# Read-back additions inside and behind the last pair's first product, and more PSUM banks for the one-hot products

## The chip, the cores and the metric

The kernel runs on one core of a Trainium2 chip. The metric is the device time of one execution, in microseconds (us); lower is better. All times below count from the start of the profiled span. The engines are named as the profile names them: PE (TensorE, matrix products), DVE (VectorE), ACT (ScalarE), POOL (GpSimd) and SP (SyncE, which here issues most of the transfers).

## The reference

A trunk of two layers works on 512 tokens of width 1024. A layer first mixes tokens (attention, pooling and a dilated attention), and then adds a mixture of experts. The change lies in the second part. Each token goes to two of 32 experts:

```python
top_v, top_i = lax.top_k(el_sel, TOP_K)
top_w = jax.nn.softmax(top_v, axis=-1) * g_w[:, None]
...
for g in range(N_GROUPS):
    hid = jax.nn.silu(jnp.einsum('td,edf->tef', t, w1[g])) * jnp.einsum('td,edf->tef', t, w3[g])
    hid = hid * combine[:, g, :, None].astype(hid.dtype)
    y = y + jnp.einsum('tef,efd->td', hid, w2[g]).astype(jnp.float32)
...
x = x + ga2 * hier_moe(h, w_rg[l], b_rg[l], w_re[l], b_re[l], w1[l], w3[l], w2[l])
```

An expert has a hidden width of 256. The reference computes in float32.

## The kernel before, in words

The token tiles X[0] to X[3] (128 tokens each) stay on the chip. In the mixture, the 32 experts are worked on in 16 pairs (pair 0 to pair 15); a pair takes up to 64 tokens for each of its two experts, so one block of 128 slots. Per pair, PE does the first product (`stage1`, L1118: eight steps j, each over two experts, into bank 0 or 1), ACT applies silu (L1122), DVE multiplies in the gate and the token's weight (L1123, "gating" below), PE transposes the hidden rows (L1130), and does the second product (`down`, L1138: two halves of 512 columns into banks 2 and 3). After the first product stands a branch (L1186) for experts with more than 64 tokens; a longer list is worked on inside it.

How a pair's result reaches X differs. Pairs 0 to 12 scatter their rows to a table `y_d` in device memory, two rows per token. In pair 13, `fetch_back` (L1203) issues eight loads that bring the table back, two for each token tile, in the order of `TAIL` = 3, 0, 2, 1; and `add_back(m)` (L1208) is two DVE additions of 128x1024 that add the two loaded halves to X[m]. These are the row additions. The last three pairs (13 to 15, `direct`) don't use the table: their result is scaled (L1150) and split into a high and a low part (ACT L299, DVE L300), and PE multiplies it by a one-hot matrix `oh` (128 slots by 512 tokens, built by DVE from the slots' token numbers in L1158). `combine` returns four steps of this, one for each token tile: in a step, for each half of the columns, PE does L1164 and L1165 into a PSUM bank and DVE adds the bank to X (L1166).

The steps of pair 13 run inside the first product of pair 14, and those of pair 14 inside that of pair 15: after j = 2, 4 and 6, and the fourth behind the gating. The steps of pair 15 stand by themselves at the end of the layer. In layer 1 each of the last ones is followed by an output transfer (L1281).

In these last pairs the order on PE, ACT, DVE and POOL is the order in which the code is written; each engine takes its work in its order. In layer 0, instructions of layer 1's beginning are woven in between, among them the loads of small tables on POOL (L320, with `lam_a`), a small reduction on `lam_a` (L387 on DVE, L389 on ACT), fills (L251), and the split of the first weights (L299, L300 with 128x1024). These tables use buffers that the read-back rows had: `lam_a` has the one of tile 0's rows (`unit_173` in layer 0).

Of the kernel before, what the change touches and what calls it, by code (L numbers as in the profile page):

```python
# [79 lines left out]
def trunk(ctx: ExitStack, tc: tile.TileContext, I, out, dbg=None):  # L80
# [46 lines left out]
    slot_f = smallp.tile([128, 2, 16, 8], F32, name="slot_f")  # L127
# [41 lines left out]
    def release(key):  # L169
        held.pop(key).free()  # L170
# [904 lines left out]
    def moe(l, us, done):  # L1075
# [10 lines left out]
        def gather(dst, idx):  # L1086
            nc.gpsimd.indirect_dma_start(out=dst, out_offset=None, in_=xn_d,  # L1087
                                         in_offset=bass.IndirectOffsetOnAxis(ap=idx, axis=0),
                                         bounds_check=S - 1, oob_is_err=False)
# [5 lines left out]
        def rows_T(src, dst, *then, banks=(4, 5)):  # L1095
            v = src.rearrange("p (q j) -> p j q", j=8)
            for j in range(8):
                nc.tensor.transpose(PS[banks[j // 4]][:, 128 * (j % 4):128 * (j % 4) + 128], v[:, j, :], ident)  # L1098
                if j == 3 and then:
                    then[0]()  # L1100
            for j in range(8):
                p = PS[banks[j // 4]][:, 128 * (j % 4):128 * (j % 4) + 128]
                if j < 4:
                    nc.scalar.activation(dst[:, j, :], p, AF.Identity, bias=cols[:, SH2, j:j + 1],
                                         scale=cols[:, SC2, j:j + 1])
                else:
                    nc.vector.tensor_scalar(dst[:, j, :], p, cols[:, SC2, j:j + 1], cols[:, SH2, j:j + 1],  # L1107
                                            op0=OP.mult, op1=OP.add)
            if then:
                then[1]()  # L1110

        def stage1(pr, b, xT, comb, between=(), after=(2, 4, 6)):

            ph = PS[b]
            for j in range(8):
                for r in range(2):
                    ws = get(("wg", l, 2 * pr + r, j // 4)).rearrange("p (n j f) -> p j n f", n=2, j=4)
                    nc.tensor.matmul(ph[64 * r:64 * r + 64, :], xT[:, j, 64 * r:64 * r + 64], ws[:, j % 4],  # L1118
                                     start=j == 0, stop=j == 7, tile_position=(0, 64 * r))
                if j in after and between:  # L1120
                    between.pop(0)()
            nc.scalar.activation(sil[b], ph[:, 0:256], AF.Silu)  # L1122
            nc.vector.scalar_tensor_tensor(hid[b], ph[:, 256:512], comb, sil[b], op0=OP.mult, op1=OP.mult)  # L1123
            for f in between:
                f()

        def hidden_T(b, part=(0, 1)):
            hv = hid[b].rearrange("p (q j) -> p j q", j=2)
            for j in part:
                nc.tensor.transpose(PS[b][:, 128 * j:128 * j + 128], hv[:, j, :], ident)  # L1130
                nc.scalar.activation(hidT[b][:, j, :], PS[b][:, 128 * j:128 * j + 128], AF.Copy)  # L1131

        def down(pr, b, banks=(2, 3), each=None):
            w2 = [get(("w2", l, 2 * pr + r)).rearrange("p (j n d) -> p j n d", j=2, n=2) for r in range(2)]
            for n in range(2):
                for j in range(2):
                    for r in range(2):
                        nc.tensor.matmul(PS[banks[n]][64 * r:64 * r + 64, :], hidT[b][:, j, 64 * r:64 * r + 64],  # L1138
                                         w2[r][:, j, n, :], start=j == 0, stop=j == 1, tile_position=(0, 64 * r))
                if each:  # L1140
                    each(n)


        direct = lambda pr: pr >= 16 - DIRECT
# [12 lines left out]
        def combine(b, tf, banks=(6, 7), done=None):  # L1157
            nc.vector.tensor_scalar(oh.bitcast(F32R), iota, tf, None, op0=OP.is_equal)  # L1158

            def step(m, n):  # L1160
                p = PS[banks[(2 * m + n) % len(banks)]]
                cs = slice(512 * n, 512 * n + 512)
                o = oh[:, 128 * m:128 * m + 128].bitcast(F32R)
                nc.tensor.matmul(p, o, yh[b][:, cs].bitcast(F32R), start=True, stop=False)  # L1164
                nc.tensor.matmul(p, o, yl[b][:, cs].bitcast(F32R), start=False, stop=True)  # L1165
                nc.vector.tensor_tensor(X[m][:, cs], X[m][:, cs], p, op=OP.add)  # L1166
                if done:
                    done(m, cs)
            return [lambda m=m: [step(m, n) for n in range(2)] for m in range(NT)]
# [13 lines left out]
        def extra(pr, b):  # L1183

            n = blocks(pr)
            with tc.If(n > 1, label=f"extra{l}_{pr}"):  # L1186
                more(pr, b, slot_f[:, 0, pr, 1:2], slot_f[:, 1, pr, 1:2], slot_y[:, pr, 1:2])
                with tc.If(n > 2):
                    with tc.For_i(2, n, 1) as k:
                        nc.vector.tensor_copy(cur_i[:, 0:1], slot_i[:, pr, ds(k, 1)])  # L1190
                        nc.vector.tensor_copy(cur_i[:, 1:2], slot_y[:, pr, ds(k, 1)])
                        nc.vector.tensor_copy(cur_f, slot_f[:, :, pr, ds(k, 1)])
                        gather(xg[2], cur_i[:, 0:1])
                        more(pr, b, cur_f[:, 0:1], cur_f[:, 1:2], cur_i[:, 1:2])

        back = []
        TAIL = (3, 0, 2, 1)

        def fetch_back():

            for m in TAIL:
                for c in range(2):
                    nc.sync.dma_start(back[m].ap[:, 1024 * c:1024 * c + 1024],  # L1203
                                      y_d[l][S * c + 128 * m:S * c + 128 * m + 128, :])

        def add_back(m):
            for c in range(2):
                nc.vector.tensor_tensor(X[m], X[m], back[m].ap[:, 1024 * c:1024 * c + 1024], op=OP.add)  # L1208

        def refill(pr):  # L1210

            last = not stream or stream[0][0][1] != l
            pump(17 - len(us) - len(back) if last else 6 if pr == 15 - DIRECT else 0)
# [6 lines left out]

        def pair(pr, b):
            tc.mark_branch_hint_location(f"extra{l}_{pr}", hint="LikelyTaken", engines=[mybir.EngineType.PE])
            steps = combine(1 - b, slot_f[:, 0, pr - 1, 0:1], (6, 7)) if pr and direct(pr - 1) else []
            if pr == 15:
                steps[1] = lambda s=steps[1]: (s(), add_back(TAIL[2]))
            stage1(pr, b, xgT[b], slot_f[:, 1, pr, 0:1], steps)

            extra(pr, b)
            for h in range(2):
                for r in range(2):  # L1230
                    release(("wg", l, 2 * pr + r, h))
            refill(pr)
            if pr == 16 - DIRECT:
                fetch_back()
            if pr + 1 < 16:
                gather(xg[2], slot_i[:, pr + 1, 1:2])
            if pr + 2 < 16:
                gather(xg[b], slot_i[:, pr + 2, 0:1])
            if pr + 1 < 16:
                rows_T(xg[1 - b], xgT[1 - b], lambda: hidden_T(b, (0,)), lambda: hidden_T(b, (1,)))  # L1240
            else:
                hidden_T(b)
                add_back(TAIL[3])
            down(pr, b, each=lambda n: gated(pr, b, slot_y[:, pr, 0:1], n))
            for r in range(2):
                release(("w2", l, 2 * pr + r))
            refill(pr)
            if pr == 14:
                add_back(TAIL[0])
                add_back(TAIL[1])  # L1250

        with tc.manual_schedule(engines=IN_MOE):
            for pr in range(16 - DIRECT):
                pair(pr, pr % 2)
# [5 lines left out]
        with tc.manual_schedule(engines=IN_LAST):  # L1260
            for pr in range(16 - DIRECT, 16):
                pair(pr, pr % 2)
            if l + 1 < L:
                nc.scalar.preload_act_table_set("natural_log_exp_and_others")
            for f in combine(1, slot_f[:, 0, 15, 0:1], (6, 7, 0, 4, 5, 1), done):
                f()
        for u in back:
            u.free()
# [33 lines left out]
```

## Time and profile before

| | |
|---|---|
| median of 3 runs (lowest to highest) | 1160.93 us (1160.9 to 1163.3) |
| profiled execution, its time and its span | 1162.47 us, 1160.5 us |
| PE busy | 1055.9 us, 91% of the span |
| DVE busy | 581.8 us, 50% |
| ACT busy | 359.4 us, 31% |
| POOL busy | 297.1 us, 26% |
| mean granted clock of PE | 0.972 |

The profile is of one execution. A timeline row has the start, the length, the engine, the line of the code, the operation, what it writes and reads, the shape, how many instructions were merged into the row, and in brackets how long the engine stood idle ahead of it and what it had waited for. The numbers of the buffers and banks are left out. A matrix product in float32 is issued as two instructions. Layer 0 ends at about 602, layer 1 with the span.

### The profile page before, as it was taken

How to read it: one execution, taken by the hardware profiler on the slowest of the kernel's cores; microseconds unless marked ns; L12 is line 12 of the kernel's file. 1: busy time of each engine (PE TensorE's matmuls, PEld its weight loads, DVE VectorE, ACT ScalarE, POOL GpSimd, SP SyncE). 2: the span in 40 equal slices, each digit the busy share in tenths (PEclk: the TensorE clock that was granted, in tenths of full speed). 3: DMA queues.
4: the chain of work that ended last, by engine and by line, in shares of the span. 5: the costliest groups of instructions: out<-in, count | busy, mean ns of one | idle time of the engine just before them, and what ended most of it. 6: DMA issues, size and time to landing. Idle time of an engine off the chain costs nothing. (4 is left out here: it accounts for less than half of the span.)

```text
span 1160.5 us, 15065 instructions
## 1 busy us (share of the span) xinstructions
PE 1055.9 (91%) x5152; PEld 571.9 (49%) x5152; DVE 581.8 (50%) x1315; ACT 359.4 (31%) x904; POOL 297.1 (26%) x260
## 2 busy tenths in 40 slices
PE   4999999999889999989779999999988998997975
PEld 1567666577533333333346676667763332332332
DVE  3567756778622222213584776587764221221255
ACT  2333354565311111201143333467632120120110
POOL 5655531002222221211134455110022221121100
PEclk9899999999999999999889999999989999999988
DMA  9957436816859999999976535620677999999992
GB/s 377 400 218 254 149 125 208 309 51 240 307 179 408 409 406 402 395 398 400 384 273 254 197 131 188 211 80 2 206 275 263 411 406 408 389 398 399 399 371 76
DMA packets 90909, 329.42 MB, mean 284 GB/s; under 512 B 19128, under 2 KB 23416, under 8 KB 76160
## 3 DMA queue, kind: packets, MB, share of 16 engines
q1 hardware_dynamic: 74992, 307.86, 69.6%
q0 software_dynamic: 14896, 17.50, 4.6%
q10 hardware_dynamic: 864, 2.17, 0.5%
q8 instruction: 74, 1.21, 0.4%
q14 instruction: 83, 0.68, 0.2%
HBM read 338.87 MB, written 29.93 MB: 318 GB/s over the span
## 5 line engine op out<-in xcount | busy, mean ns | idle before, releaser
L1118 PE MATMUL ps<-unit,unit 128*64 128x512 f32 x1120 | 271.5, 609 | 15.5 <-DMA unit<-w 14.8
L303 PE MATMUL ps<-unit,unit 128*128 128x512 f32 x448 | 182.6, 413 | 0.9 <-ACT unit L299 0.9
L304 PE MATMUL ps<-unit,unit 128*128 128x512 f32 x448 | 177.4, 397 | 2.8 <-POOL unit L300 1.5
L1118 PEld LDWEIGHTS ps<-unit,unit 128*64 128x64 f32 x1120 | 85.6, 140 | 186.0 <-issue 175.5
L305 PE MATMUL ps<-unit,unit 128*128 128x512 f32 x448 | 176.4, 396 | 0.5 <-DVE unit L300 0.5
L1138 PE MATMUL ps<-unit,unit 128*64 128x512 f32 x560 | 138.9, 618 | 6.5 <-ACT unit L1131 4.6
L1123 DVE SCALAR_TENSOR_TENSOR unit<-ps,slot_f,unit 128x256 f32<-128x256 f32 x35 | 16.9, 484 | 233.5 <-ACT unit L1122 233.5
L300 POOL TENSOR_TENSOR unit<-unit,unit 128x1024 fp32r<-128x1024 f32 (+1 forms) x46 | 104.9, 2284 | 100.9 <-ACT unit L299 100.9
L1122 ACT ACTIVATE unit<-ps 128x256 f32<-128x256 f32 x35 | 13.5, 384 | 371.5 <-issue 285.8
L299 ACT ACTIVATE unit<-unit 128x1024 fp32r<-128x1024 f32 (+1 forms) x92 | 87.9, 962 | 116.5 <-PE ps L305 60.8
L1087 POOL DMA_INDIRECT unit<-xn_d,slot_i x62 | 62.8, 1013 | 220.6 <-PEq L1186 160.9
L303 PEld LDWEIGHTS ps<-unit,unit 128*128 128x128 f32 x448 | 84.6, 189 | 36.6 <-issue 17.2
L304 PEld LDWEIGHTS ps<-unit,unit 128*128 128x128 f32 x448 | 84.9, 190 | 22.4 <-DVE unit L300 3.5
L305 PEld LDWEIGHTS ps<-unit,unit 128*128 128x128 f32 x448 | 84.3, 189 | 19.4 <-DVE unit L300 1.2
L1138 PEld LDWEIGHTS ps<-unit,unit 128*64 128x64 f32 x560 | 36.1, 139 | 82.8 <-issue 46.9
L1153 DVE TENSOR_TENSOR unit<-ps,unit 128x512 f32<-128x512 f32 x58 | 40.1, 692 | 72.1 <-PE ps L1138 72.1
L1092 POOL DMA_INDIRECT y_d<-unit,slot_y x29 | 29.6, 1021 | 171.2 <-DVE unit L1153 96.2
L535 ACT ACTIVATE unit<-unit,sm 128x512 f32<-128x512 f32 (+3 forms) x96 | 53.2, 555 | 32.9 <-DVE sm L533 32.4
L311 ACT ACTIVATE unit<-ps 128x512 f32<-128x512 f32 (+3 forms) x84 | 40.6, 490 | 70.6 <-PE ps L305 22.9
L1107 DVE TENSOR_SCALAR unit<-ps,cols 128x128 f32<-128x128 f32 x132 | 45.1, 404 | 31.4 <-PE ps L1098 31.1
L300 DVE TENSOR_TENSOR unit<-unit,unit 128x1024 fp32r<-128x1024 f32 (+1 forms) x46 | 54.9, 1198 | 11.7 <-ACT unit L299 11.1
L309 DVE COPY unit<-ps 128x512 f32<-128x512 f32 (+3 forms) x80 | 43.8, 552 | 31.8 <-PE ps L524 12.3
(223 smaller groups left out, 1346.0 us busy)
## 6 DMA issues: line engine op xcount, KB each, us to landing
unit<-w SPq DMA_DIRECT2D x256, 512.0 KB, 13.3
unit<-w SPq DMA_DIRECT2D x64, 1024.0 KB, 13.2
unit<-w_mod SPq DMA_DIRECT2D x48, 1024.0 KB, 7.0
unit<-w_in SPq DMA_DIRECT2D x16, 1024.0 KB, 14.9
y_d<-k_zero SPq DMA_DIRECT2D x16, 512.0 KB, 10.3
unit<-w_out SPq DMA_DIRECT2D x8, 1024.0 KB, 4.9
unit<-y_d SPq DMA_DIRECT2D x16, 512.0 KB, 10.7
unit<-w_in SPq DMA_DIRECT2D x8, 512.0 KB, 4.7
```

Of the source, the lines that this page charges most:

```text
L299: nc.scalar.activation(hi.bitcast(F32R), src, AF.Copy)
L300: (eng or nc.gpsimd).tensor_tensor(lo.bitcast(F32R), src, hi, op=OP.subtract)
L303: nc.tensor.matmul(o, ahi.bitcast(F32R), bhi.bitcast(F32R), start=first, stop=False)
L304: nc.tensor.matmul(o, ahi.bitcast(F32R), blo.bitcast(F32R), start=False, stop=False)
L305: nc.tensor.matmul(o, alo.bitcast(F32R), bhi.bitcast(F32R), start=False, stop=last)
L309: nc.vector.tensor_copy(dst, src)
L311: nc.scalar.activation(dst, src, AF.Copy)
L535: nc.scalar.activation(dst[:, :n], dst[:, :n], AF.Exp, bias=mx, scale=-1.0, accum_out=z)
L1087: nc.gpsimd.indirect_dma_start(out=dst, out_offset=None, in_=xn_d, in_offset=bass.IndirectOffsetOnAxis(ap=idx, axis=0), bounds_check=S - 1 ...
L1107: nc.vector.tensor_scalar(dst[:, j, :], p, cols[:, SC2, j:j + 1], cols[:, SH2, j:j + 1], op0=OP.mult, op1=OP.add)
L1118: nc.tensor.matmul(ph[64 * r:64 * r + 64, :], xT[:, j, 64 * r:64 * r + 64], ws[:, j % 4], start=j == 0, stop=j == 7, tile_position=(0, 64 ...
L1138: nc.tensor.matmul(PS[banks[n]][64 * r:64 * r + 64, :], hidT[b][:, j, 64 * r:64 * r + 64], w2[r][:, j, n, :], start=j == 0, stop=j == 1, t ...
```

## The change

Three things are done, in both layers. The steps of pair 13 use four PSUM banks (6, 7, 2, 3) and those of pair 14 six (6, 7, 2, 3, 4, 5), where both had used 6 and 7. The row additions of tiles 3 and 0, which stood behind pair 14's second product, now stand behind the second and third step inside pair 15's first product; those of tiles 2 and 1, of which one stood behind the second step and one behind pair 15's transposes, now both stand behind the transposes. And the steps of pair 15 are made ahead of these additions and of the second product, and run, as before, at the end; making them builds `oh`, so L1158 stands earlier on DVE.

```diff
         back = []
         TAIL = (3, 0, 2, 1)
+        tail = []
...
-            steps = combine(1 - b, slot_f[:, 0, pr - 1, 0:1], (6, 7)) if pr and direct(pr - 1) else []
+            steps = combine(1 - b, slot_f[:, 0, pr - 1, 0:1], (6, 7, 2, 3, 4, 5)[:6 if pr == 15 else 4]) if pr and direct(pr - 1) else []
             if pr == 15:
-                steps[1] = lambda s=steps[1]: (s(), add_back(TAIL[2]))
+                for k in (1, 2):
+                    steps[k] = lambda s=steps[k], m=TAIL[k - 1]: (s(), add_back(m))
             stage1(pr, b, xgT[b], slot_f[:, 1, pr, 0:1], steps)
...
                 hidden_T(b)
-                add_back(TAIL[3])
+                tail.extend(combine(b, slot_f[:, 0, pr, 0:1], (6, 7, 0, 4, 5, 1), done))
+                for m in TAIL[2:]:
+                    add_back(m)
             down(pr, b, each=lambda n: gated(pr, b, slot_y[:, pr, 0:1], n))
...
             refill(pr)
-            if pr == 14:
-                add_back(TAIL[0])
-                add_back(TAIL[1])
...
-            for f in combine(1, slot_f[:, 0, 15, 0:1], (6, 7, 0, 4, 5, 1), done):
+            for f in tail:
                 f()
```

One line is added above them, so that lines behind it count one more in the changed kernel (L1208 is L1209 there).

The order on DVE in layer 1, from pair 14's last split to pair 15's gating (X[0] and X[1] lie in `unit_1_170`, X[2] and X[3] in `unit_2_171`; `unit_339`, `336` and `338` are the loaded rows of tiles 3, 0 and 2; `ps_142` to `147` are banks 2 to 7). Before:

```order
L300 TENSOR_TENSOR unit_335_10811<-ps_143,unit_334_10810 128x512
L1208 TENSOR_TENSOR unit_2_171<-unit_2_171,unit_339_10815 128x1024 x2
L1208 TENSOR_TENSOR unit_1_170<-unit_1_170,unit_336_10812 128x1024 x2
L1158 TENSOR_SCALAR oh<-unit_3_172,slot_f 128x512
L1166 TENSOR_TENSOR unit_1_170<-unit_1_170,ps_146 128x512
L1166 TENSOR_TENSOR unit_1_170<-unit_1_170,ps_147 128x512
L1166 TENSOR_TENSOR unit_1_170<-unit_1_170,ps_146 128x512
L1166 TENSOR_TENSOR unit_1_170<-unit_1_170,ps_147 128x512
L1208 TENSOR_TENSOR unit_2_171<-unit_2_171,unit_338_10814 128x1024 x2
L1166 TENSOR_TENSOR unit_2_171<-unit_2_171,ps_146 128x512
L1166 TENSOR_TENSOR unit_2_171<-unit_2_171,ps_147 128x512
L1123 SCALAR_TENSOR_TENSOR unit_258_8079<-ps_141,slot_f,unit_3_172 128x256
```

and in the changed kernel:

```order
L300 TENSOR_TENSOR unit_335_10811<-ps_143,unit_334_10810 128x512
L1158 TENSOR_SCALAR oh<-unit_3_172,slot_f 128x512
L1166 TENSOR_TENSOR unit_1_170<-unit_1_170,ps_146 128x512
L1166 TENSOR_TENSOR unit_1_170<-unit_1_170,ps_147 128x512
L1166 TENSOR_TENSOR unit_1_170<-unit_1_170,ps_142 128x512
L1166 TENSOR_TENSOR unit_1_170<-unit_1_170,ps_143 128x512
L1209 TENSOR_TENSOR unit_2_171<-unit_2_171,unit_339_10815 128x1024 x2
L1166 TENSOR_TENSOR unit_2_171<-unit_2_171,ps_144 128x512
L1166 TENSOR_TENSOR unit_2_171<-unit_2_171,ps_145 128x512
L1209 TENSOR_TENSOR unit_1_170<-unit_1_170,unit_336_10812 128x1024 x2
L1123 SCALAR_TENSOR_TENSOR unit_258_8079<-ps_141,slot_f,unit_3_172 128x256
```

`oh` has come up to the split, the row additions have gone behind the second and the third step, with the second of them right ahead of the gating, and tile 2's have left this stretch.

The order on DVE in layer 0 behind pair 15's branch, as a difference (`unit_175` and `174` are the rows of tiles 2 and 1, `unit_195` the buffer of layer 1's small tables, `unit_183` and `196` the first weights of layer 1 and their split):

```order
-L1208 TENSOR_TENSOR unit_1_170<-unit_1_170,unit_174_5155 128x1024 x2
+L1158 TENSOR_SCALAR oh<-unit_3_172,slot_f 128x512
+L1209 TENSOR_TENSOR unit_2_171<-unit_2_171,unit_175_5156 128x1024
+L251 MEMSET unit_195_6002 128x512
+L1209 TENSOR_TENSOR unit_2_171<-unit_2_171,unit_175_5156 128x1024
+L1209 TENSOR_TENSOR unit_1_170<-unit_1_170,unit_174_5155 128x1024
+L251 MEMSET unit_195_6002 128x512
+L1209 TENSOR_TENSOR unit_1_170<-unit_1_170,unit_174_5155 128x1024
 L1150 TENSOR_TENSOR ps_142<-ps_142,unit_3_172 128x512
+L387 SCALAR_TENSOR_TENSOR unit_194_6001,lamt<-unit_195_6002 128x64 x2
+L300 TENSOR_TENSOR unit_196_6003<-unit_183_5936,unit_196_6003 128x1024
 L300 TENSOR_TENSOR unit_172_5153<-ps_142,unit_171_5152 128x512
```

`oh` stands ahead of four row additions where two stood, and L387, which in the kernel before stands behind the second L1150, now stands behind the first, ahead of both splits of pair 15.

The order on POOL in layer 0 around the load of `lam_a`. Before:

```order
L320 DMA unit_195_6002<-gk_c 128x64
L320 DMA unit_195_6002<-lam_a 128x256
L252 DMA unit_195_6002<-b_mod 4x512 x2
L1181 TENSOR_LOAD nblk
L1186 COMPARE_AND_BRANCH
```

and in the changed kernel:

```order
L1186 ISA
L1186 UNCONDITIONAL_BRANCH
L320 DMA unit_195_6002<-lam_a 128x256
L409 DMA unit_189_5996<-k_rope 128x512
L374 DMA unit_189_5996<-k_band 128x1536
L252 DMA unit_195_6002<-b_mod 4x512
```

The load has moved behind pair 15's branch, whose end is L1186 in the second piece.

## Rows read from the trace of the kernel before

**Rows 1.** The one line `oh` (L1158), who waited for it (us, times), whole span

```profile
  PE ps L1164: 18.5, 4
```

**Rows 2.** Timeline, PE, layer 1 (start us, us, engine, line, op, names, shape, count, [idle before <- releaser])

```profile
1125.84 0.77 PE L1164 MATMUL ps<-unit,oh 128*128 128x512 f32 x1 [6.25 <-DVE oh L1158]
...
1130.24 0.49 PE L1164 MATMUL ps<-unit,oh 128*128 128x512 f32 x1
...
1133.24 0.50 PE L1164 MATMUL ps<-unit,oh 128*128 128x512 f32 x1
...
1135.54 0.50 PE L1164 MATMUL ps<-unit,oh 128*128 128x512 f32 x1
...
1140.20 0.46 PE L1130 MATMUL ps<-ident,unit 128*128 128x128 f32 x1 [3.34 <-PEq L1186]
...
1141.44 5.93 PE L1138 MATMUL ps<-unit,unit 128*64 128x512 f32 x16
```

**Rows 3.** Timeline, DVE, layer 1

```profile
1118.79 0.69 DVE L300 TENSOR_TENSOR unit<-ps,unit 128x512 fp32r<-128x512 f32 x1 [0.72 <-ACT unit L299]
1120.22 5.07 DVE L1208 TENSOR_TENSOR unit<-unit,unit 128x1024 f32<-128x1024 f32 x4 [0.74 <-DMA unit<-y_d]
1125.21 0.48 DVE L1158 TENSOR_SCALAR oh<-unit,slot_f 128x512 fp32r<-128x512 f32 x1
...
1131.01 1.28 DVE L1166 TENSOR_TENSOR unit<-unit,ps 128x512 f32<-128x512 f32 x2 [2.41 <-PE ps L1165]
...
1136.40 1.27 DVE L1166 TENSOR_TENSOR unit<-unit,ps 128x512 f32<-128x512 f32 x2
1137.98 2.48 DVE L1208 TENSOR_TENSOR unit<-unit,unit 128x1024 f32<-128x1024 f32 x2 [0.31 <-DVEq L1186]
1145.17 0.70 DVE L1150 TENSOR_TENSOR ps<-ps,unit 128x512 f32<-128x512 f32 x1 [4.71 <-PE ps L1138]
1146.59 0.69 DVE L300 TENSOR_TENSOR unit<-ps,unit 128x512 fp32r<-128x512 f32 x1 [0.72 <-ACT unit L299]
...
1153.01 3.68 DVE L1166 TENSOR_TENSOR unit<-unit,ps 128x512 f32<-128x512 f32 x6 [0.17 <-PE ps L1165]
```

**Rows 4.** Stretches: busy us PE, PEld, DVE, ACT, POOL (counts), PEclk, DMA share, GB/s

```profile
1132.00:1134.00 2.00, 2.00 (x11) 0.81 (x6) 1.97 (x3) 0.00 (x0) 0.00 (x0) 1.00 0.04 16
...
1142.00:1144.00 2.00, 2.00 (x6) 0.47 (x4) 0.00 (x0) 0.00 (x0) 0.00 (x0) 0.50 0.00 0
```

**Rows 5.** Branch L1186 on PE's queue, all pairs (ns min/median/max)

```profile
L1186 PEldq COMPARE_BRANCH  x32: 74/358/6237, 321.4 to 1136.5; - x32
```

**Rows 6.** Timeline, SP's queue, the last issues

```profile
1152.02 5.03 SPq L1281 DMA_DIRECT2D out<-unit  x8
```

**Rows 7.** Timeline, PE, layer 0

```profile
573.54 0.76 PE L1164 MATMUL ps<-unit,oh 128*128 128x512 f32 x1 [5.61 <-DVE oh L1158]
...
587.25 3.65 PE L1138 MATMUL ps<-unit,unit 128*64 128x512 f32 x16
```

**Rows 8.** Timeline, DVE, layer 0

```profile
567.73 3.61 DVE L1208 TENSOR_TENSOR unit<-unit,unit 128x1024 f32<-128x1024 f32 x3
571.77 1.23 DVE L1208 TENSOR_TENSOR unit<-unit,unit 128x1024 f32<-128x1024 f32 x1 [0.43 <-DMA unit<-y_d]
572.91 0.48 DVE L1158 TENSOR_SCALAR oh<-unit,slot_f 128x512 fp32r<-128x512 f32 x1
...
592.05 0.22 DVE L387 SCALAR_TENSOR_TENSOR unit<-unit 128x64 f32<-128x64 f32 x1
...
596.08 0.69 DVE L1166 TENSOR_TENSOR unit<-unit,ps 128x512 f32<-128x512 f32 x1 [0.86 <-PE ps L1165]
```

**Rows 9.** Timeline, POOL, layer 0

```profile
575.44 0.54 POOL L320 DMA_DIRECT2D unit<-lam_a  x1
```

**Rows 10.** DMA issues in 560 to 600 (count, KB each, us to landing)

```profile
unit<-lam_a POOLq DMA_DIRECT2D x1, 128.0 KB, 8.7
```

**Rows 11.** Timeline, ACT, layer 0

```profile
592.85 1.28 ACT L1264 ACT_TABLE_LOAD   x1
```

## The prediction

> **What bounds the kernel now.** I read the waits first. The one-hot table `oh` (L1158) is what the PE's one-hot products (L1164, L1165) wait for, 18.5 us in four waits [rows 1]. Two of the four lie ahead of the last pair's steps: 6.25 us in layer 1 [rows 2] and 5.61 us in layer 0 [rows 7]. The timelines of DVE say why. `oh` is cheap (0.48 us), but DVE takes its work in order, and four additions of read-back rows (L1208) stand ahead of it: 1120.22 to 1125.29 in layer 1, `oh` at 1125.21, PE's product 0.63 us behind its start [rows 2, 3]; 567.73 to 573.00 in layer 0 [rows 8]. The other two waits lie at the layers' ends, where `oh` of pair 15 is built behind all the splits. During the first wait the PE's clock falls, so the group that follows (one step and eight L1118) lasts 4.40 us (1125.84 to 1130.24) where the next lasts 3.00 [rows 2].
>
> The transfers set the pace up to about 1130; at 1132 to 1134 the DMA share is 0.04 and 16 GB/s [rows 4], so nothing that this change brings forward in layer 1 can run into missing data for long. Pair 15's last weights are the latest; the second product would reach them at 1134.1 (below).
>
> **The change, layer 1.** No addition is added or dropped: 16 of L1208 stay 16 in the two layers, one costs about 1.2 us (two in 2.48 [rows 3]). They trade places with `oh`, and the steps take banks 2 to 5 beside 6 and 7.
>
> `oh` now stands right behind the split at 1118.79, which with 0.60 us of spacing gives 1119.39, 5.82 us earlier. Step 0 starts 0.63 later, at 1120.02, with so short a pause (the wait of 6.25 us began at 1119.59) that I take the faster clock: groups of 3.00 put step 1 at 1123.02 and step 2 at 1126.02; step 3 follows 2.30 later (1135.54 less 1133.24), at 1128.32 [rows 2].
>
> DVE's additions to X begin 0.77 us behind a step (1131.01 less 1130.24), a pair of them taking 1.20 [rows 2, 3]. Step 1's: 1123.79 to 1124.99. The rows of tile 3: to 1127.40. They need data that in the trace had landed at 1120.22; tile 0's were added by 1125.29 [rows 3], so both are in place. Step 2's additions to 1128.60, tile 0's rows to 1131.00. The gating of the hidden rows (L1123), which in the order stands behind this, is late by some 2.2 us against its input. That is the wait which the change adds; the transposes of PE are queued behind it. In layer 1 it is covered: PE itself stands in the branch L1186 until 4.66 us behind step 3's start (1140.20 less 1135.54), of which 3.34 is the branch [rows 2]. So the transposes come at about 1132.9, after the gated rows (1131.4), and the second product (L1138) at 1134.1.
>
> DVE meanwhile: step 3's additions from 1131.4; 1.58 later (1137.98 less 1136.40 [rows 3]) the new `oh`; then the last four row additions, 4.8 us, until 1138.2. In the trace of before two of these stood there. [...] So L1150 starts at about 1138.2 by DVE, and 1137.9 by PE. It stood at 1145.17: 7.0 us gained.
>
> Behind it the tail is shorter too. L1150 and split follow one another in 1.42 and 0.60 us (L1150 at 1145.17, L300 at 1146.59 [rows 3]): the second split starts at 1138.2 + 1.42 + 0.60 + 1.42 = 1141.6 and ends at 1142.3. `oh` no longer follows it, and the first step's first product has run by then. The first addition is at 1142.3, the second waits for its product until about 1143.0, and seven at 0.60 end at 1147.3; they ended at 1156.69 (1153.01 + 3.68). That is 9.4 us at the last addition. The eight output transfers get their first tile 9.0 earlier (issued at 1152.02 [rows 6], now at about 1143.0) and are then packed a little tighter, so I take **9.2 us** for layer 1.
>
> **Layer 0** has the same steps, but another engine's loads stand in the way. `oh` moves from 572.91 to 567.73, 5.18 us; step 0 to 568.36 [rows 7, 8]. The same spacings give: step 1's additions 572.13, tile 3's rows to 575.7, step 2's to 576.9, tile 0's rows to 579.4, gating 579.4, `oh` 581.3, the last four row additions and two fills (an estimate of 0.5 each, from `oh`, which has the same shape) until 587.5, L1150 until 588.1. There L387 is next, the small reduction on layer 1's `lam_a`, in the order now ahead of both splits. `lam_a` is loaded into the buffer that holds tile 0's rows, so its load starts only when these have been added. In the trace they ended at 573.00 (571.77 + 1.23), `lam_a` was issued at 575.44 and took 8.7 [rows 8 to 10]: it landed 11.1 us behind the addition. With the addition ending at 579.4 that is 590.5; the load also stands behind POOL's branch now, so I take 591.0. L387 stood at 592.05. Behind it stands the same work as before (two splits, L1150, the weight's split), and the first addition followed 4.03 us later (596.08). So of about 5 us that PE gains, **1.0 us** is left in layer 0; DVE waits some 2.9 us on `lam_a`.
>
> The sides of this cost: with `lam_a` there at once, L387 starts at 588.2 and the gain is 592.05 less 588.2, 3.9, less some 0.3 for the splits' order: 3.6. If POOL's branch adds as much as PE's did in layer 1 (3.3 us [rows 2]), it starts at 593.8 and 1.8 is lost. I stay near the row, since this is the same load on the same crowded engines.
>
> [...]
>
> An extra table load of ACT (1.28 us, as the one at 592.85 [rows 11]) comes in ahead of `lam_a`'s exponential. I cost it at nothing, since it runs while DVE waits and splits; without that cover it would reach 590.8, still ahead of what needs it. The banks: step 1 writes banks 2 and 3 after the split at 1118.79 has read them, step 2 banks 4 and 5 after the transposed rows were read; in pair 14 step 3's additions empty banks 2 and 3 ahead of the second product, with the transposes between. I cost these at nothing; if one were late, a pair of additions, 1.2 us, would show.
>
> **Sum.** 9.2 + 1.0 = 10.2 us. The profiled execution took 1162.47 with a span of 1160.5, which would become 1152.3; the median of the runs is 1160.93, so the forecast for it is 1150.7.
>
> **The rivals.**
> - The loads come early: `lam_a` ahead of 588.2. For it speaks that its own packets are few; against it the 8.7 us. Gain 9.2 + 3.6 = 12.8, 1148.1. [...]
> - More is given back: `lam_a` at 593.8 (layer 0 loses 1.8), or the PE's branch in the last pair takes not 3.4 but the longest seen, 6.2 us [rows 5], which puts L1138 2.8 later and L1150 2.5 later than DVE allows. Gain 7.4, or with both 4.9: 1153.5 to 1156.0.
> - Slower than before: the wait on `lam_a` in front of everything in layer 0. Every microsecond beyond 592.05 is lost one for one; it eats layer 1's 9.2 at 601.3, that is with 21.9 us from the addition to the landing instead of 11.1. At 24.5 the time is 1163.5. Twice the 8.7 us that the load took would be needed, which speaks against it; that DVE, ACT and PE all stand behind it speaks for it.
> - It doesn't do what it says: DVE stands on the first row addition with the gating behind it, because tile 3's rows land late. It would have to be after 1125.0 to cost anything, 4.8 us behind the 1120.22 of the trace; at 9 us behind that the gain is gone and the time about 1160.
>
> **How the numbers follow.** Forecast 0.60, with its own range 1149.0 to 1152.5; early loads 0.15; more given back 0.17; slower 0.03; no effect 0.05. The range that leaves out no more than 2 in 10 takes in the whole first case and most of the next two: 1147.6 to 1154.6. About 0.2% (2.3 us) is what a measurement of this kernel can tell from no change. The first three cases all are faster by more than that: 0.92; within it 0.05, slower 0.03.
>
> **What would show it.** In the new trace: no wait of L1164 on `oh` ahead of pair 15's steps, and L1164 of step 0 within 0.7 us of the split; steps 3.0 us apart at clock 1.00; L1123 directly behind the row additions; in layer 1 L1150 with DVE busy right up to it, within 0.5 us of L1138's first half, and its end about 9 us nearer to pair 14's last split; in layer 0 DVE idle ahead of L387 with `lam_a` as the releaser, some 3 us, and the first addition 4.0 us behind it. The forecast is wrong if L387 doesn't wait (then more is gained), if PE waits more than 3.5 us for the gating, or if layer 1's L1138 waits for weights beyond 1135.

## The result: 15 us faster, 3.7 us beyond the forecast

The first comparison gave 1146.98 us (median of four runs, 1145.57 to 1148.20) against 1162.12 us (four runs, 1160.90 to 1165.18): a ratio of 0.9861, with an interval of 0.9836 to 0.9886. The forecast was 1150.7 us, with 1147.6 at the low end. A second comparison with more runs (6 against 17) gave 1148.76 against 1161.95, a ratio of 0.9887 (0.9863 to 0.9910), that is 13.2 us. The first median lies 0.6 us below the forecast's low end, the second inside its range and 1.9 us below the forecast itself.

The profiled execution of the changed kernel took 1146.14 us, with a span of 1144.2 (before: 1162.47 and 1160.5). Three stretches hold what the change touches (outside them lie only the other banks of pair 13's steps in layer 1). They are marked by instructions of VectorE (DVE), so that each can be measured in any trace:

- A, layer 0: from the second L1150 of pair 13 to the first L1150 of pair 14. In it lies pair 14's second product.
- B, layer 0: from the second L1150 of pair 14 to the first L1166 of the last product.
- C, layer 1: from the second L1150 of pair 14 to the end of the span.

"Rest" is the span less A, B and C. All values are us; the runs are told below.

| kernel | A | B | C | A+B+C | rest |
|---|---|---|---|---|---|
| before | 20.36 | 30.37 | 43.09 | 93.82 | 1066.64 |
| before, second trace (before2) | 21.97 | 29.04 | 43.36 | 94.37 | 1064.32 |
| changed | 17.85 | 28.92 | 34.25 | 81.02 | 1063.20 |
| changed, second trace (again) | 17.96 | 29.31 | 33.51 | 80.78 | 1065.20 |
| rows | 20.44 | 28.24 | 33.84 | 82.52 | 1067.12 |
| banks | 16.76 | 33.34 | 38.28 | 88.38 | 1064.89 |
| pair14_67 | 20.88 | 28.13 | 34.18 | 83.18 | 1066.94 |
| layer0 | 16.94 | 29.25 | 42.89 | 89.07 | 1064.75 |
| layer1 | 20.32 | 28.65 | 33.51 | 82.48 | 1069.77 |
| lam_late | 17.81 | 32.92 | 34.29 | 85.02 | 1064.36 |
| oh_late | 18.16 | 36.51 | 35.14 | 89.81 | 1064.84 |
| pool_rows | 17.68 | 28.86 | 32.47 | 79.01 | 1067.55 |
| pool_early | 17.41 | 29.44 | 33.49 | 80.33 | 1065.00 |
| spread | 16.78 | 29.13 | 32.62 | 78.53 | 1065.92 |

So in these three stretches the change is worth about 13 us (93.8 or 94.4 less 81.0 or 80.8). The spans of the first two profiled executions differ by 16.2 because the rest was 3.4 us shorter as well. It moves by 6.6 us between these 14 traces, and that of the changed kernel is the shortest of them.

Layer 1's end went as forecast. The one line `oh` and who waited for it, in the changed kernel (the four waits of [rows 1] are three short ones now):

```profile
  PE ps L1164: 1.2, 3
```

TensorE (PE) in layer 1's last pair, changed kernel, to set beside [rows 2] (start, us, engine, line, ..., count, [idle before <- releaser]):

```profile
1112.61 0.47 PE L1164 MATMUL ps<-unit,oh 128*128 128x512 f32 x1 [0.43 <-DVE oh L1158]
...
1120.72 0.50 PE L1164 MATMUL ps<-unit,oh 128*128 128x512 f32 x1
...
1124.07 0.48 PE L1130 MATMUL ps<-ident,unit 128*128 128x128 f32 x1 [2.16 <-DVE unit L1123]
...
1125.34 5.38 PE L1138 MATMUL ps<-unit,unit 128*64 128x512 f32 x16
```

And DVE there, to set beside [rows 3]:

```profile
1121.15 2.47 DVE L1209 TENSOR_TENSOR unit<-unit,unit 128x1024 f32<-128x1024 f32 x2
1123.54 0.48 DVE L1123 SCALAR_TENSOR_TENSOR unit<-ps,slot_f,unit 128x256 f32<-128x256 f32 x1
...
1125.83 4.87 DVE L1209 TENSOR_TENSOR unit<-unit,unit 128x1024 f32<-128x1024 f32 x4
1130.62 0.69 DVE L1150 TENSOR_TENSOR ps<-ps,unit 128x512 f32<-128x512 f32 x1
...
1134.06 0.69 DVE L300 TENSOR_TENSOR unit<-ps,unit 128x512 fp32r<-128x512 f32 x1 [0.72 <-ACT unit L299]
1134.66 0.68 DVE L1166 TENSOR_TENSOR unit<-unit,ps 128x512 f32<-128x512 f32 x1
```

PE waits 0.43 us for the table ahead of step 0. The gating L1123 stands right behind the row additions and is what PE waits for. DVE works up to L1150 without a pause, and the first addition of the last product follows the last split at once.

Layer 0 did not go as forecast. PE in pair 14's second product of layer 0, first before and then changed:

```profile
558.81 1.07 PE L1138 MATMUL ps<-unit,unit 128*64 128x512 f32 x2
561.76 3.16 PE L1138 MATMUL ps<-unit,unit 128*64 128x512 f32 x13 [1.88 <-issue]
```

```profile
557.47 4.04 PE L1138 MATMUL ps<-unit,unit 128*64 128x512 f32 x16
```

Before, PE did two of the 16 matmuls and then nothing that the trace explains ("issue") until 561.76. The transfers went on meanwhile: from 558.9 to 561.7 the DMA share was 1.04, at 400 GB/s. This stop is gone. It lies ahead of anything that moving rows or the table could reach.

Later in layer 0, DVE and the transfer of `lam_a` in the changed kernel (for [rows 8] and [rows 10]):

```profile
584.66 0.70 DVE L1150 TENSOR_TENSOR ps<-ps,unit 128x512 f32<-128x512 f32 x1 [1.32 <-PE ps L1138]
586.59 0.23 DVE L387 SCALAR_TENSOR_TENSOR unit<-unit 128x64 f32<-128x64 f32 x1 [1.24 <-PE ps L1138]
```

```profile
unit<-lam_a POOLq DMA_DIRECT2D x1, 128.0 KB, 5.8
```

`lam_a`, issued at 579.90, took 5.8 us instead of 8.7 and was there at 585.7. L387 then waited for the end of PE's product at 586.56, not for the load. That product, pair 15's second one, was itself late. It began 9.2 us earlier than before, but now it waited twice for its weights and lasted 8.5 us instead of 3.65 [rows 7]:

```profile
578.06 1.96 PE L1138 MATMUL ps<-unit,unit 128*64 128x512 f32 x2 [0.93 <-DMA unit<-w]
580.95 5.61 PE L1138 MATMUL ps<-unit,unit 128*64 128x512 f32 x14 [0.93 <-DMA unit<-w]
```

### The profile page after: what moved, and what is told of

Same layout as the page of the kernel before. It is cut to its first block, busy times and chain, and to the rows that moved or that the text cites. A ratio compares the mean times of both kernels' runs of the same rounds, so it can differ in the third digit from the quotient of the medians.

```text
span 1144.2 us, 15074 instructions
## 1 busy us (share of the span) xinstructions
PE 1049.7 (92%) x5152; PEld 567.3 (50%) x5152; DVE 581.1 (51%) x1315; ACT 360.1 (31%) x905; POOL 296.7 (26%) x260
## 3 DMA queue, kind: packets, MB, share of 16 engines
q8 instruction: 74, 1.21, 0.4%
## 5 line engine op out<-in xcount | busy, mean ns | idle before, releaser
L1138 PE MATMUL ps<-unit,unit 128*64 128x512 f32 x560 | 140.3, 616 | 6.6 <-ACT unit L1131 2.3
L1123 DVE SCALAR_TENSOR_TENSOR unit<-ps,slot_f,unit 128x256 f32<-128x256 f32 x35 | 16.9, 484 | 237.0 <-ACT unit L1122 237.0
L300 POOL TENSOR_TENSOR unit<-unit,unit 128x1024 fp32r<-128x1024 f32 (+1 forms) x46 | 104.8, 2282 | 101.2 <-ACT unit L299 101.1
L1138 PEld LDWEIGHTS ps<-unit,unit 128*64 128x64 f32 x560 | 36.5, 139 | 84.0 <-issue 42.6
L300 DVE TENSOR_TENSOR unit<-unit,unit 128x1024 fp32r<-128x1024 f32 (+1 forms) x46 | 54.9, 1198 | 11.6 <-ACT unit L299 11.0
```

The lines of the kernel that those rows point to most:

```text
L300: (eng or nc.gpsimd).tensor_tensor(lo.bitcast(F32R), src, hi, op=OP.subtract)
```

## The experiments

All ratios are against runs of the kernel before on the same chip, with 95% intervals.

**The changed kernel again, and each layer alone.** `again` has no edit. `layer1` and `layer0` make the change in one layer:

```
+        NEW = l == 1          # layer1;  l == 0 for layer0
... the new banks, the moved rows and the early table where NEW, the old code elsewhere
```

> The changed kernel once more, against the kernel before. Two theories of the 5.9 us by which the first result (16.3 us between the spans of the two profiled executions, 15.1 between the medians) went past the forecast of 10.2. Theory A, scatter: 10.2 us belong to the change (8.9 measured in layer 1's end, 1.3 in layer 0's end), and the rest (1.35 us ahead of the first changed instruction, 2.5 us of a transfer that was late in pair 14 of layer 0 in the trace of before alone, 2.3 us of slow-clock stretches at 863 and 981 us in the trace of before alone) is not the change's and would fall elsewhere in another execution: gain in this round 10 to 13 us, and a trace with late weights or slow stretches at other places. Theory B, all of it belongs to the change: gain 15 to 16.5 us again, and the trace has neither the late weights in pair 14 nor the slow stretches.

> The change in layer 1 alone; layer 0 and layer 1 up to pair 13 issue the same instructions as before. Theory A: 8.9 us faster than before, plus or minus 2 of scatter, with layer 0's last pair as in the trace of before (first addition of rows 5.6 to 6.3 us behind pair 14's split pattern, PE waiting about 5.6 us for the table); whether the late weights of pair 14 and the slow stretches at 863 and 981 stand there is chance, and says how much of the first 1100 us moves without any change. Theory B: 8.9 us at the end, and everything ahead of 1100 us as in the trace of before to within 0.3 us, with all three delays there.

> The change in layer 0 alone; layer 1 as before. My forecast for this part was 1.0 us, with lam_a's landing as what L387 waits for. Theory A: 1.0 to 2.0 us faster than before, plus or minus 2 of scatter; first addition to X of the last product 1.3 us earlier against pair 14's last split than a trace with that pair's weights late would give. Theory B: the loads come early, so that L387 waits for the PE's product and not for lam_a: 3.7 us or more, and with the slow stretches of layer 1's front gone too up to 7.4 us.

Measured: `again` 0.9887 (0.9863 to 0.9910), 13.2 us between the medians. `layer1` 0.9942 (0.9916 to 0.9967), 7.8 us. `layer0` 0.9950 (0.9931 to 0.9968), 5.3 us. The two parts add up (13.1). C falls by 9.6 to 9.9 us with layer 1's part alone, and A by 3.4 or more with layer 0's. The gain of `again` fits neither range: it is just above theory A's 10 to 13 and below theory B's 15 to 16.5.

Theory A (only 10.2 us are the change's) was half right. Part of the surplus is scatter: `layer1`, whose first 1100 us issue the same instructions as before, has the longest rest of all. But theory B's signs held too. The slow-clock stretches of the expectation are in both traces of before (mean granted clock 0.74 and 0.61 in 860 to 873, 0.81 and 0.81 in 979 to 988) and in neither of the changed kernel (1.00 in all four). They are no gain, though: from layer 0's first L1166 of the last product to layer 1's second L1150 of pair 13 it is 501.2 and 500.3 us before, 501.1 and 502.8 in the changed kernel. And the stop in pair 14 is not chance. Its length in A is there in `layer1` and absent in `layer0` and `again`. So something in the change removes it, and the rows and the table cannot. That left the banks.

**The banks.** `rows` is the changed kernel without them, `banks` is the kernel before with them alone, and `pair14_67` takes them away for one set of steps:

```
 rows:       combine(1 - b, ..., (6, 7))                                       # changed kernel otherwise
 banks:      combine(1 - b, ..., (6, 7, 2, 3, 4, 5)[:6 if pr == 15 else 4])    # kernel before otherwise
 pair14_67:  combine(1 - b, ..., (6, 7, 2, 3, 4, 5)[:6 if pr == 15 else 2])    # changed kernel otherwise
```

> The changed kernel with all steps on banks 6 and 7, as before: the rows and the table are moved, the banks aren't. Theory C: the banks let PE's own queue run ahead. With two banks the loads of step 3 wait until step 2's additions have emptied a bank, and the queue behind them (the branch L1186, and with it the fetch of the instructions behind the branch) waits too; with four or six banks it passes the branch 4.4 us earlier in layer 0's pair 14. So here the stop of 2.9 us in pair 14's second product of layer 0 (before: two L1138 at 558.81, the next at 561.76) comes back, the branch of pair 15 in layer 1 starts behind step 3's loads instead of some 4 us ahead of them and takes 3.3 to 6.5 us, so that L1130 comes 0.9 to 4 us later: in all 3.4 to 6.5 us slower than the changed kernel, 7 to 10 us faster than before. Theory D: the stop's absence comes with other code addresses and the banks do nothing: as the changed kernel within 1 us (12 to 14 us faster than before).

> The kernel before with the banks of the change alone (four for pair 13's steps, six for pair 14's); rows and table stay where they were. Theory C: the stop of 2.9 us in pair 14's second product of layer 0 is gone, of which the additions of rows, which wait for their data there until 571.7, leave 0.5 to 1 us; in layer 1 the branch of pair 15 is passed before the steps' end, so that the 3.3 us in which PE stood in it are gone: 3 to 5 us faster than before. Theory D, and my forecast, which costed the banks at nothing: as before within 1 us.

> The changed kernel with pair 13's steps (they run inside pair 14's first product) on banks 6 and 7 instead of four banks; pair 15 keeps its six. Theory C: the branch of pair 14 in layer 0 is reached behind step 2's additions again, 4.4 us later than in the changed kernel, the instruction fetch starts when PE has run out, and PE stops for 2.5 to 3 us in pair 14's second product; some 2.5 us slower than the changed kernel if the wait for the second product's weights in pair 15 does not take up part of it, 1.5 if it does. Theory D: no stop, within 0.5 us of the changed kernel.

Measured: `rows` 0.9914 (0.9897 to 0.9931), 10.5 us faster than before. `banks` 0.9966 (0.9949 to 0.9983), 4.8 us. `pair14_67` 0.9924 (0.9906 to 0.9943), 9.3 us. The stop came back in the two kernels where pair 13's steps use two banks. PE in `rows`, then in `pair14_67`, then in `banks`:

```profile
556.49 1.07 PE L1138 MATMUL ps<-unit,unit 128*64 128x512 f32 x2
559.46 3.16 PE L1138 MATMUL ps<-unit,unit 128*64 128x512 f32 x13 [1.90 <-issue]
```

```profile
557.66 1.07 PE L1138 MATMUL ps<-unit,unit 128*64 128x512 f32 x2
560.90 4.80 PE L1138 MATMUL ps<-unit,unit 128*64 128x512 f32 x13 [2.17 <-issue]
```

```profile
556.51 4.04 PE L1138 MATMUL ps<-unit,unit 128*64 128x512 f32 x16
```

The mechanism shows on PE's own queue. The load of the block count (L1181) and the branch (L1186) stand in it behind the steps. Before, then changed, 545 to 560 us (ns min/median/max, first and last start):

```profile
L1181 PEldq TENSOR_LOAD <-nblk x1: 306/306/306, 555.8 to 555.8; - x1
L1186 PEldq COMPARE_BRANCH  x1: 328/328/328, 556.2 to 556.2; - x1
```

```profile
L1181 PEldq TENSOR_LOAD <-nblk x1: 305/305/305, 551.5 to 551.5; - x1
L1186 PEldq COMPARE_BRANCH  x1: 328/328/328, 551.9 to 551.9; - x1
```

With two banks, step 3 has to wait until step 2's additions have emptied a bank, and the queue stands with it; with four it takes the banks that step 1's additions have emptied. The times fit in all 14 traces: the load of the block count starts 0.05 us behind the end of these additions (before, step 2's end at 555.75 and the load starts at 555.80; changed, step 1's end at 551.40 and the load starts at 551.45). With four banks PE's queue reaches the branch 5.6 us ahead of the product's first L1138, with two 2.6 us ahead (557.47 less 551.9; 558.81 less 556.2). What follows the branch is seen among the transfers: a 16 KB packet on the queue of kind "instruction" (in the profile of before, q8 has 74 packets with 1.21 MB in all). Before, in 558.9 to 561.7 us (PE's stop), then changed, in 554.9 to 556.4 (ahead of the product):

```profile
q8 instruction: 1, 0.02, 2.0%
```

```profile
q8 instruction: 1, 0.02, 4.2%
```

In all 14 traces this packet starts 3.0 to 4.1 us behind the branch. The first L1138 comes 2.6 to 2.7 us behind the branch in the five traces with two banks, so that the product begins ahead of the packet, and 5.6 us behind it in the nine with more. The five have the stop and the nine do not. In the five, PE's matmuls go on 2.5 to 2.7 us behind the start of the packet, and in `before2`, where the packet came latest (4.0 us behind the branch, against 3.0 to 3.3 in the other four), the stop was the longest. That the banks make the stop is shown by `pair14_67`; that PE lacks instructions during it is read from these times and was not tried by itself.

Not everything expected of the banks held. In `rows` I expected 3.4 to 6.5 us lost against the changed kernel: its A+B+C is only 1.5 to 1.7 longer, and its gain of 10.5 us is 2.7 below that of `again`. `pair14_67` lost 2.2 to 2.4 us in A+B+C, where 1.5 to 2.5 were expected, but its gain is 3.9 us below that of `again`. In `rows` PE stood 3.74 us in the branch again in layer 1, but DVE had work up to L1150 anyway, so C stayed at 33.84. In `banks` layer 0 gives nearly all of A's gain back in B (33.34), where DVE waits three times for read-back rows (2.8 us in sum) ahead of its table. Its 4.8 us come from layer 1, where PE is through the branch in time:

```profile
1134.15 0.36 PE L1130 MATMUL ps<-ident,unit 128*128 128x128 f32 x1 [0.15 <-PEq L1186]
```

**`lam_a` made late.** The read-back buffers are given back in another order:

```
-        for u in back:
-            u.free()
+        for m in (1, 0, 2, 3):
+            back[m].free()
```

> The changed kernel with the read-back buffers given back in another order, so that layer 1's gains and lam_a are loaded into the buffer of tile 1's rows (the last ones added, until about 583.3) instead of tile 0's (until 575.5). It tests the step of my forecast that put lam_a's landing ahead of everything in layer 0. If DVE's order behind L387 makes it so, lam_a is issued at about 587 and lands at 593 (5.8 us, as in the changed kernel), L387 starts there instead of at 586.6, and the kernel is 5 to 7 us slower than the changed one. Rival: the wait is covered by the PE's product and by w_in's splits, and at most 1 us is lost.

Measured: 0.9922 (0.9903 to 0.9940), 9.8 us faster than before, some 4 us slower than the changed kernel (3.4 by the gains, 4.0 to 4.2 in A+B+C), between the 5 to 7 that I expected and the rival's 1. B grew by 3.6 to 4.0. DVE:

```profile
593.83 0.29 DVE L387 SCALAR_TENSOR_TENSOR unit<-unit 128x64 f32<-128x64 f32 x1 [3.76 <-DMA unit<-lam_a]
```

So the wait that I feared exists, and with this order of the buffers it costs time. The loss is less than the 7 us by which L387 is later, since both splits had been done ahead of it here.

**The table late again.**

```
-                tail.extend(combine(b, slot_f[:, 0, pr, 0:1], (6, 7, 0, 4, 5, 1), done))
...
-            for f in tail:
+            for f in combine(1, slot_f[:, 0, 15, 0:1], (6, 7, 0, 4, 5, 1), done):
```

> The changed kernel with the table oh of pair 15 built behind all splits again, as before; rows and banks as changed. My theory: in the changed kernel the first addition of the last product follows the last split at once (1134.66 behind 1134.06 in layer 1); here the table (0.6 us of spacing), the wait of the PE's first product for it (0.43) and two products with the way back to VectorE (0.9) stand between: first addition some 1.7 us later in each layer, 3.0 to 3.5 us slower than the changed kernel, and a wait of L1164 on oh ahead of the last product in both layers. Rival: the first product's other operand, the low half, comes last anyway (L1165 waits for L300), so that only 0.6 us are lost in each layer.

Measured: 0.9960 (0.9943 to 0.9977), 4.4 us faster than before, about 9 us slower than the changed kernel. Layer 1 lost 0.9 to 1.6 (C), near the 1.7. Layer 0 lost 7.2 to 7.6 (B), which neither theory had. DVE there:

```profile
590.80 6.55 DVE L1158 TENSOR_SCALAR oh<-unit,slot_f 128x512 fp32r<-128x512 f32 x1
```

The table took 6.55 us instead of 0.48, while GpSimd worked nearly without a gap on layer 1's tables (L380, L383, L300) until 597.1. In the kernel before it took 0.50 us at 594.20, when this work had just begun (593.69). Why it took so little there and so much here is open; building it early takes it out of the way.

**Against what bounds the changed kernel.** In layer 1, DVE's row additions reach up to L1150. `pool_rows` and `pool_early` give some of them to GpSimd, `spread` puts them into DVE's pauses:

```
 pool_rows:   for m in TAIL[2:]: add_back(m, nc.gpsimd)          # layer 1
 pool_early:  steps 0 and 2: add_back(0 and 1, nc.gpsimd); step 1: add_back(3); behind the table: add_back(2)
 spread:      half tiles: 1 behind step 0, 2 behind step 1, 1 each behind steps 2 and 3, 3 behind the table
```

> The changed kernel with the last four row additions of layer 1 (tiles 2 and 1) on GpSimd instead of VectorE. My theory of layer 1's end is that L1150 there is bound by VectorE, which is busy with these four up to it (1125.83 to 1130.70). Then L1150 comes when PE's first half is ready, 2.5 to 3 us behind the product's start at 1125.34, that is at about 1128.1, and the kernel gains 2 to 2.5 us over the changed one. GpSimd's own 128x1024 operations take 2.28 us each, four of them 9.1 us from about 1121, done by 1130.5, ahead of the additions that need tiles 1 and 2. Rival: GpSimd and VectorE get in one another's way, or GpSimd ends later than 1134: no gain, or slower by up to 3 us.

> The changed kernel with layer 1's rows shared out: GpSimd adds tile 0's behind step 0 and tile 1's behind step 2 of the last pair, ahead of the branch that held GpSimd until 1129 in the run pool_rows; VectorE adds tile 3's behind step 1 and tile 2's behind the table. GpSimd's additions took 2.4 us each there. My theory: L1150 of the last pair then comes with the PE's first half, 3.75 us behind the product's start, 18.7 us behind pair 14's second L1150 instead of 20.65; the end comes 1.5 to 2.4 us earlier than in the changed kernel. Rival: GpSimd's work slows VectorE down (the table took 2.55 us beside it in pool_rows, 0.49 without) or ends too late for the last additions: no gain.

> The changed kernel with layer 1's eight half tiles of rows spread so that VectorE's pauses take some: one behind step 0 (VectorE stood 1.71 us there until step 1's product), two behind step 1, one each behind steps 2 and 3, three behind the table instead of four. My theory (VectorE is what bounds L1150 of the last pair in the changed kernel): no pause is left, the gating comes 1.2 us earlier but PE is held by the branch until about 13.7 us behind pair 14's second L1150, L1150 comes 1.0 to 1.3 us earlier against that L1150 (20.65 to about 19.5) and the end with it; in the times 1.2 us are within what five rounds can tell. Rival: the first half tile has not landed behind step 0, VectorE stands and step 1's additions, and with them the gating, come later: no gain, or a loss of up to 1 us.

Measured: `pool_rows` 0.9879 (0.9854 to 0.9904), `pool_early` 0.9883 (0.9858 to 0.9908), `spread` 0.9861 (0.9833 to 0.9890). None can be told from the changed kernel by time. Their traces say more. Against the changed kernel's two traces C is 1.0 to 1.8 us shorter in `pool_rows`, where 2 to 2.5 were expected, 0.0 to 0.8 shorter in `pool_early`, where 1.5 to 2.4 were expected, and 0.9 to 1.6 shorter in `spread`. In `pool_rows` the branch of DVE held GpSimd until 1129.47, and the last additions then waited for GpSimd:

```profile
1129.47 9.61 POOL L1209 TENSOR_TENSOR unit<-unit,unit 128x1024 f32<-128x1024 f32 x4 [20.22 <-DVEq L1186]
```

In `pool_early` two of DVE's row additions took 6.39 us instead of 2.48 beside GpSimd's:

```profile
1119.43 6.39 DVE L1209 TENSOR_TENSOR unit<-unit,unit 128x1024 f32<-128x1024 f32 x2
```

`spread` did what was expected: L1150 came 19.1 us behind pair 14's second one (1130.97 less 1111.83) instead of 20.65, and its A+B+C is the shortest of all. That is 2.3 to 2.5 us below the changed kernel's, of which the scatter of A alone may be one; the times do not resolve it.

**A second trace of before.**

> The kernel before once more, for a second trace of it. Theory C (banks): PE stops again for 2.5 to 2.8 us in pair 14's second product of layer 0, and stands in the branch of pair 15 in layer 1 for some 3.3 us; both are the program's. Scatter: the start of layer 0 may be up to 1.8 us off, and the slow-clock stretches at 863 and 981 us may be missing.

One run, 1160.69 us. The stop in pair 14 and the stand in layer 1's branch (3.35 us) were both there again, as theory C says; A+B+C is within 0.6 us of the first trace, and the slow-clock stretches are there again as well, which the expectation had left to chance.

## Why the prediction was wrong

**Layer 1, 9.2 us: right.** C fell from 43.1 and 43.4 to 34.25 and 33.5, that is by 8.8 to 9.9. The single steps held too: the table at once behind the split, steps 3.00 apart, the gating right behind the rows, L1150 bound by DVE. One did not hold, though L1150's bound stayed the same. I took the branch to cover the late gating, in the old place behind step 3. With six banks PE's queue reached it 3.5 us ahead of step 3, so that it ended at 1123.7, and PE waited for the gating. The branch in the changed kernel, 1105 to 1141 us:

```profile
L1186 PEldq COMPARE_BRANCH  x1: 6493/6493/6493, 1117.2 to 1117.2; - x1
```

No run shows the 1137.9 us by PE that stands beside DVE's 1138.2: in the changed kernel DVE held L1150 until 5.28 us behind L1138's start (1130.62 less 1125.34), and where L1150 waited for PE it came 3.73 us behind it in the trace of before (1145.17 less 1141.44), 3.75 in `pool_rows` and 3.73 in `pool_early`.

**The failed step: "The banks: ... I cost these at nothing; if one were late, a pair of additions, 1.2 us, would show."** I asked only whether a bank is free when a product needs it. I did not ask what stands on PE's queue behind the instruction that waits for the bank. That was the branch, and behind it the instructions of the next product. The banks are worth about 3 us in A (20.3 to 22.0 with two, 16.8 to 18.2 with more), some 1 us of which B takes back (28.1 to 28.2 in `rows` and `pair14_67`, 28.9 to 29.3 in `changed` and `again`). The stop was in the trace of before as 1.88 us of "issue" in pair 14's second product, a place that I had not read. Without the banks, `rows` gave 10.5 us where I forecast 10.2 for the whole.

**Layer 0, 1.0 us through `lam_a`: the mechanism is real, but the forecast had no term for PE's weights.** In `rows`, which has the moved rows and the table but not the banks, L387 waited 1.99 us where I forecast 2.9. The profile names PE's L1164 there, but that one had begun at 586.48, and `lam_a` landed at 587.4, 0.1 us before L387 started. B fell there by 0.8 to 2.1 against the two traces of before. With the banks PE reaches pair 15's second product earlier, its weights do not come as much earlier, and the product ends later than the load: in the changed kernel `lam_a` was there 0.9 us ahead of its end. That holds in five of the six traces with the changed kernel's layer 0 (`changed`, `again`, `layer0`, `pool_early`, `spread`). In the sixth, `pool_rows`, the load came last:

```profile
588.48 0.22 DVE L387 SCALAR_TENSOR_TENSOR unit<-unit 128x64 f32<-128x64 f32 x1 [2.14 <-DMA unit<-lam_a]
```

The rival of early loads came nearest, with 1148.1, and its condition held (`lam_a` ahead of 588.2). But that is in part luck: its 3.6 us of layer 0 would lie in B, and B fell by 1.5 at most, while 2.4 to 4.1 of layer 0's gain lie in A, where the rival has nothing.

**The remainder is open.** Of the 16.2 us between the first two spans, 12.8 lie in A, B and C. Of the other 3.4, 2.0 lie in layer 1 between pair 13's second L1150 and pair 14's first: 18.1 us before, 16.1 in the changed kernel, and 17.8 and 16.0 in the second traces. Before, PE waits for weights there:

```profile
1098.47 2.76 PE L1118 MATMUL ps<-unit,unit 128*64 128x512 f32 x10 [0.68 <-DMA unit<-w]
```

All five traces with two banks in this stretch have this wait (17.8 to 18.3 us). Of the nine with four, `layer1`, `lam_late`, `oh_late` and `pool_rows` have it too (17.9 to 18.3), and five do not (16.0 to 16.5). The wait lies ahead of the first step there that uses another bank, so these banks do not make it by themselves. Whether something earlier in the change does, through the transfers, no run shows; if it does, the change is worth up to 2 us more than A, B and C say. What is left, 1.4 us, has the other sign between the second traces (the changed kernel 2.7 us longer), and is scatter.

## What to carry to other kernels

When an instruction waits for a buffer, list what is queued behind it on its own engine, with branches and the instructions behind them, and not only who needs its result: a bank that is free in time for the product may still hold up the queue (here, in pair 14 of layer 0, PE reached the branch at 556.2 us with two banks and at 551.9 with four). A stop put down to "issue" just behind a branch is worth a look at the instruction queue among the transfers. And before a saving of one or two us is explained, measure by marks the stretch that the edit touches, since the untouched rest moved by more than that.

## What the runs showed of the hardware

- A 16 KB packet on the instruction queue starts 3.0 to 4.1 us behind PE's branch of pair 14, in 14 of 14 traces; when the product reaches the place first, PE stops, and its matmuls go on 2.5 to 3.5 us behind the last, and 2.5 to 2.7 us behind the packet's start (five of five).
- DVE beside GpSimd: L1158 (0.48 us alone) took 2.55 us in `pool_rows` and 6.55 in `oh_late`, and two row additions (2.48) took 6.39 in `pool_early`. In `pool_rows` a pair of L1166, which reads one operand from PSUM, took 1.36 us beside GpSimd's additions, against 1.28 elsewhere. The 6.55 us span some ten GpSimd operations and not one (590.23 to 597.07). By what means DVE is slower beside GpSimd, no run shows.
